# Rotary embedding, 1 core: all loads and stores on SyncE's one queue, in a written-out order

## The chip, the cores and the metric

The kernel runs on 1 core of one Trainium2 chip. The metric is the device time of an execution in microseconds (us). The program uses five engines: TensorE (PE), VectorE (DVE), ScalarE (ACT), GpSimd (POOL) and SyncE (SP). Transfers between HBM and SBUF are run by the core's 16 DMA engines; SP and ACT each issue theirs on a queue of their own (q1 is SP's in the profile, q10 is ACT's).

## The reference

```python
# x [8, 2048, 8, 64], cos and sin [2048, 32], all float32
def reference(x, cos, sin):
    x1 = x[..., : x.shape[-1] // 2]
    x2 = x[..., x.shape[-1] // 2 :]
    cos = cos[None, :, None, :]
    sin = sin[None, :, None, :]
    out1 = x1 * cos - x2 * sin
    out2 = x1 * sin + x2 * cos
    return np.concatenate([out1, out2], axis=-1)
```

x is 33.55 MB and so is the output; each table is 0.26 MB.

## The kernel before

The 2048 positions of a batch are laid over 128 partitions, 16 positions (`R`) to a partition, so that one batch is one tile `xt` of 128 x 8192 float32 (4 MB, `ROW` elements in a partition). `HD` is 512 elements (one position of all heads) and `UNIT` is 2048 (four positions). There are 8 batches and `NBUF` = 5 tiles: batches 0 to 4 are loaded ahead, and the load of batch 5 has to wait until the store of batch 0 has left its tile, that of 6 for the store of 1, that of 7 for the store of 2. Results are written back into the tile they came from, and stored from there. In the following, x5 stands for the load of batch 5 and s5 for its store.

`load` (L64) issues the loads on SP's queue: batch 0 in pieces of 1, 1 and 2 MB with the cos table behind the first of them (L69), every other batch in one transfer of 4 MB (L67). The sin table is loaded on ACT's queue (L76). `store` (L72) issues stores on ACT's queue (L74), those of the last batch on SP's. A queue's instructions are issued in the order of the program; where a transfer waits for a semaphore, all that its engine has behind it waits too. The names `keep(...)` put an instruction at its place in that order.

`rotate` (L102) works on one piece of a batch, mostly a `UNIT` (128 x 2048), and has three kinds. Kind A: GpSimd multiplies with sin and with minus sin (L122, two instructions of 128 x 1024), VectorE multiplies with cos (L129) and adds (L136). Kind B (first piece of batches 2, 4 and 5): the same products, the sum is made by TensorE with an identity matrix into PSUM (L143, L144) and copied back by ACT (L145). Kind C (first piece of batches 1 and 3): VectorE makes both products (L129, L148), TensorE the sums (L160, L161), ACT the copies (L165). The cos table is first copied to PSUM by VectorE (L93), sin to its negative and to PSUM by ACT (L90, L91).

The loop at L184 takes the batches in turn. `pieces` (L170) gives the pieces of a batch, `shares` (L177) how its store is cut: batch 0 into 512, 3584 and 4096 elements of a partition, the last batch into 4096, 2048 and 2048, the others whole. After batch b the load of batch b + 5 is issued:

```python
        if b + NBUF <= last:
            load(b + NBUF)
```

Of the kernel before, what the change touches and what calls it, by code (L numbers as in the profile page):

```python
# [10 lines left out]
def kernel(  # L11
# [7 lines left out]
    nc = tc.nc  # L19
    keep = tc.keep_in_program_order  # L20
# [6 lines left out]
    HD = H * D  # L27
    R = S // P
    ROW = R * HD
    UNIT = 4 * HD  # L30
    NBUF = 5
    C = 512
    last = B - 1

    xv = x.rearrange("b (q r) h d -> b q (r h d)", q=P)
    ov = out.rearrange("b (q r) h d -> b q (r h d)", q=P)
    cos_src = cos.rearrange("(q r) d -> q r d", q=P)
    sin_src = sin.rearrange("(q r) d -> q r d", q=P)
# [10 lines left out]
    sin_sb = const_pool.tile([P, R, Dh], f32, tag="sb")  # L49
# [6 lines left out]
    xts = {}  # L56

    def spans(sizes):
        lo = 0
        for n in sizes:  # L60
            yield lo, n
            lo += n

    def load(b):  # L64
        xt = xpool.tile([P, ROW], f32, tag="xt", name=f"xt{b}")
        for lo, n in spans([UNIT, UNIT, 2 * UNIT] if b == 0 else [ROW]):
            keep(nc.sync.dma_start(out=xt[:, lo : lo + n], in_=xv[b, :, lo : lo + n]))  # L67
            if b == 0 and lo == 0:
                keep(nc.sync.dma_start(out=cos_sb, in_=cos_src))  # L69
        xts[b] = xt  # L70

    def store(b, lo, n):  # L72
        queue = nc.sync if b == last else nc.scalar
        keep(queue.dma_start(out=ov[b, :, lo : lo + n], in_=xts[b][:, lo : lo + n]))  # L74

    keep(nc.scalar.dma_start(out=sin_sb, in_=sin_src))  # L76
    for b in range(NBUF):
        load(b)

# [2 lines left out]
        out=eye,  # L82
        in_=eye,
# [86 lines left out]
    def pieces(b):  # L170
        if b == 0:
            return [2 * HD, 2 * HD, UNIT, UNIT, UNIT]
        if b == last:
            return [UNIT, UNIT, UNIT, 2 * HD, 2 * HD]
        return [UNIT] * 4

    def shares(b):  # L177
        if b == 0:
            return [HD, 7 * HD, 2 * UNIT]
        if b == last:  # L180
            return [2 * UNIT, UNIT, UNIT]
        return [ROW]

    for b in range(B):  # L184
        done = 0
        outs = list(spans(shares(b)))
        for lo, n in spans(pieces(b)):
            rotate(b, lo, n)
            done = lo + n
            while outs and sum(outs[0]) <= done:  # L190
                store(b, *outs.pop(0))
        if b + NBUF <= last:
            load(b + NBUF)


# [28 lines left out]
```

## Time and profile before

| what | value |
|---|---|
| time, median of 3 runs | 163.59 us (163.51 to 164.44) |
| profiled execution: span from the first to the last instruction | 161.6 us (2.0 us below the median of the runs; no other time is listed for it) |
| busy: VectorE, GpSimd | 140.1 us (87%), 138.9 us (86%) |
| busy: TensorE, ScalarE | 47.1 us (29%), 12.8 us (8%) |
| moved by DMA | 67.65 MB, mean 419 GB/s over the span |
| time of the packets on 16 engines: SP's queue, ACT's queue | 55.3% of the span (38.01 MB), 42.9% (29.62 MB) |
| a load of 4 MB, issue to landing (median of 7) | 40.3 us |
| a store of 4 MB on ACT's queue, issue to landing (median of 6) | 28.3 us |

Busy shares are shares of the span. The time from issue to landing of a transfer holds the time it stands behind others in its queue and shares the engines with the other queue; it is not the time that its bytes need. The span is compared with spans, and the time with times.

### The profile page before, as it was taken

The page shows a single profiled execution, that of the slowest core. Times are in us where ns is not written, and L with a number is a line of the kernel's source. Part 1 is how long each engine was busy: PE and PEld are TensorE (multiplying, and loading weights), DVE is VectorE, ACT ScalarE, POOL GpSimd, SP SyncE. Part 2 cuts the span into 40 slices and gives each one's busy share as a digit, 9 for nine tenths or more (in the row PEclk, how much of TensorE's full clock was granted, in tenths as well). Part 3 has the DMA queues.
Part 4 walks back from the last instruction along what each step waited for, and adds up shares of the span by engine and source line. Part 5 has one row for each costly group of instructions (what it writes and reads, how often), then busy time and mean ns, then how long its engine had stood idle before and what let it go on. Part 6 is the DMA issues. An engine that isn't in the chain of part 4 may idle for free.

```text
span 161.6 us, 460 instructions
## 1 busy us (share of the span) xinstructions
PE 47.1 (29%) x80; PEld 17.8 (11%) x80; DVE 140.1 (87%) x66; ACT 12.8 (8%) x14; POOL 138.9 (86%) x70
## 2 busy tenths in 40 slices
PE   0000000597209750977039813972000000000000
PEld 0000000143004210322023302330000000000000
DVE  0297999999999999999999999699969999899920
ACT  3300000002200220022000120022000000000000
POOL 1399999999999999976999989997899979999500
PEclk9999999999965997599858995699555555555555
DMA  5999999999999999999999999999999999999995
GB/s 157 419 462 413 424 469 403 394 457 457 410 402 450 442 470 389 454 454 389 470 438 389 471 432 389 462 446 398 446 448 406 430 462 406 430 462 397 414 408 225
DMA packets 3458, 67.65 MB, mean 419 GB/s; under 512 B 384, under 2 KB 384, under 8 KB 768
## 3 DMA queue, kind: packets, MB, share of 16 engines
q1 hardware_dynamic: 2016, 38.01, 55.3%
q10 hardware_dynamic: 1440, 29.62, 42.9%
q14 instruction: 2, 0.02, 0.0%
HBM read 34.08 MB, written 33.55 MB: 419 GB/s over the span
## 4 chain that ended last, share of the span: by engine, by line
DVE 53%; DMA 29%; POOL 9%; issue 5%; DVEq 0%; SPq 0%; POOLq 0%
DVE t L129 28%; DMA xt<-in_x_dram 25%; DVE xt L136 22%; POOL t L122 9%; DMA sin_sb<-in_sin_dram 4%; DVE t L148 3%; DVEq L136 0%; SPq L67 0%; POOLq L122 0%
## 5 line engine op out<-in xcount | busy, mean ns | idle before, releaser
L122 POOL TENSOR_TENSOR t<-xt,sin_sb 128x1024 f32<-128x1024 f32 (+1 forms) x32 | 70.5, 2202 | 12.1 <-DMA xt<-in_x_dram 6.7
L129 DVE TENSOR_TENSOR t<-xt,cos_ps 128x2048 f32<-128x2048 f32 (+1 forms) x34 | 73.4, 2166 | 0.8
L122 POOL TENSOR_TENSOR t<-xt,nsin 128x1024 f32<-128x1024 f32 (+1 forms) x32 | 70.5, 2202 | 0.0
L136 DVE TENSOR_TENSOR xt<-t,t 128x2048 f32<-128x2048 f32 (+1 forms) x29 | 62.2, 2144 | 6.7 <-POOL t L122 4.1
L143 PE MATMUL o<-t,eye 128*128 128x512 f32 x24 | 15.9, 749 | 24.4 <-DVE t L129 21.0
L160 PE MATMUL o<-t,eye 128*128 128x512 f32 x16 | 11.2, 789 | 38.3 <-DVE t L129 36.1
L144 PE MATMUL o<-t,eye 128*128 128x512 f32 x24 | 14.7, 698 | 0.0
L145 ACT COPY xt<-o 128x1024 f32<-128x1024 f32 x6 | 6.1, 1012 | 45.7 <-PE o L144 45.7
L143 PEld LDWEIGHTS o<-t,eye 128*128 128x128 f32 x24 | 5.3, 247 | 33.6 <-issue 27.7
L160 PEld LDWEIGHTS o<-t,eye 128*128 128x128 f32 x16 | 3.7, 256 | 43.8 <-POOL t L122 30.2
L165 ACT COPY xt<-o 128x1024 f32<-128x1024 f32 x4 | 4.0, 1012 | 47.3 <-PE o L161 47.3
L93 DVE COPY cos_ps<-cos_sb 128x512 f32<-128x512 f32 x1 | 0.7, 694 | 7.0 <-DMA cos_sb<-in_cos_dram 7.0
L144 PEld LDWEIGHTS o<-t,eye 128*128 128x128 f32 x24 | 5.4, 227 | 7.4 <-issue 7.4
L161 PE MATMUL o<-t,neye 128*128 128x512 f32 x8 | 6.2, 863 | 0.2 <-DVE t L148 0.2
L148 DVE TENSOR_TENSOR t<-xt,sin_ps 128x2048 f32<-128x2048 f32 x2 | 4.6, 2280 | 0.0
L161 PE MATMUL o<-t,eye 128*128 128x512 f32 x8 | 4.1, 592 | 0.0
L161 PEld LDWEIGHTS o<-t,neye 128*128 128x128 f32 x8 | 1.8, 260 | 4.7 <-issue 3.0
L161 PEld LDWEIGHTS o<-t,eye 128*128 128x128 f32 x8 | 1.5, 190 | 1.9 <-issue 1.9
L90 ACT ACT_TABLE_LOAD x1 | 1.3, 1283 | 1.2 <-PEq L208 1.2
L90 ACT ACTIVATE nsin<-sin_sb 128x512 f32<-128x512 f32 x1 | 0.6, 630 | 4.1 <-DMA sin_sb<-in_sin_dram 4.1
L91 ACT COPY sin_ps<-sin_sb 128x512 f32<-128x512 f32 x1 | 0.6, 579 | 0.0
L80 POOL MEMSET eye<- 128x128 f32 x1 | 0.2, 205 | 0.3 <-POOLq L208 0.3
(6 smaller groups left out, 1.0 us busy)
## 6 DMA issues: line engine op xcount, KB each, us to landing
xt<-in_x_dram SPq DMA_DIRECT2D x7, 4096.0 KB, 40.3
out_dram<-xt ACTq DMA_DIRECT2D x6, 4096.0 KB, 28.3
xt<-in_x_dram SPq DMA_DIRECT2D x2, 1024.0 KB, 6.7
xt<-in_x_dram SPq DMA_DIRECT2D x1, 2048.0 KB, 12.4
out_dram<-xt ACTq DMA_DIRECT2D x1, 2048.0 KB, 25.9
out_dram<-xt SPq DMA_DIRECT2D x1, 2048.0 KB, 11.1
out_dram<-xt SPq DMA_DIRECT2D x2, 1024.0 KB, 7.5
out_dram<-xt ACTq DMA_DIRECT2D x1, 1792.0 KB, 20.8
```

Of the source, the lines that this page charges most:

```text
L90: keep(nc.scalar.mul(nsin, sin_sb, -1.0))
L93: keep(nc.vector.tensor_copy(cos_ps, cos_sb))
L122: nc.gpsimd.tensor_mul(out=t2u[:, :, u, :].rearrange("p (r h) d -> p r h d", h=H), in0=xu[:, :, 1 - u, :].rearrange("p (r h) d -> p r h d" ...
L129: nc.vector.tensor_mul(out=t1.rearrange("p (r k d) -> p r k d", r=nr, d=Dh), in0=xk, in1=rep(cos_ps[:, r0 : r0 + nr, :], 2 * H),)
L136: keep(nc.vector.tensor_add(out=xt, in0=t1, in1=t2))
L143: nc.tensor.matmul(oc, eye, t1[:, cs], start=True, stop=False)
L144: nc.tensor.matmul(oc, eye, t2[:, cs], start=False, stop=True)
L145: keep(nc.scalar.copy(xt[:, 2 * j * C : 2 * (j + 1) * C], o))
L148: nc.vector.tensor_mul(out=t2.rearrange("p (r k d) -> p r k d", r=nr, d=Dh), in0=xk, in1=rep(sin_ps[:, r0 : r0 + nr, :], 2 * H),)
L160: nc.tensor.matmul(oc, eye, t1u[:, gs, u, :], start=True, stop=False)
L161: nc.tensor.matmul(oc, eye if u else neye, t2u[:, gs, 1 - u, :], start=False, stop=True)
L165: nc.scalar.copy(xu[:, :, u, :], o.rearrange("p (g d) -> p g d", d=Dh))
```

## The change

The sin table is loaded on SP's queue, between the first piece of x and the cos table. All stores go to SP's queue. Batch 0 is stored by one transfer of 4 MB instead of three. The loads of batches 5, 6 and 7 are issued one batch later in the loop: after batch b (from 1 on) comes the load of batch b + 4, so that on SP's queue s1 stands ahead of x5, s2 ahead of x6 and s3 ahead of x7. The order of the other engines' arithmetic stays; ACT has no transfers left. Lines after L75 move up by one.

```diff
         for lo, n in spans([UNIT, UNIT, 2 * UNIT] if b == 0 else [ROW]):
             keep(nc.sync.dma_start(out=xt[:, lo : lo + n], in_=xv[b, :, lo : lo + n]))
             if b == 0 and lo == 0:
+                keep(nc.sync.dma_start(out=sin_sb, in_=sin_src))
                 keep(nc.sync.dma_start(out=cos_sb, in_=cos_src))
         xts[b] = xt
 
     def store(b, lo, n):
-        queue = nc.sync if b == last else nc.scalar
-        keep(queue.dma_start(out=ov[b, :, lo : lo + n], in_=xts[b][:, lo : lo + n]))
-
-    keep(nc.scalar.dma_start(out=sin_sb, in_=sin_src))
+        keep(nc.sync.dma_start(out=ov[b, :, lo : lo + n], in_=xts[b][:, lo : lo + n]))
+
     for b in range(NBUF):
         load(b)
...
     def shares(b):
         if b == 0:
-            return [HD, 7 * HD, 2 * UNIT]
+            return [ROW]
         if b == last:
             return [2 * UNIT, UNIT, UNIT]
         return [ROW]
...
             while outs and sum(outs[0]) <= done:
                 store(b, *outs.pop(0))
-        if b + NBUF <= last:
-            load(b + NBUF)
+        if b >= 1 and b + NBUF - 1 <= last:
+            load(b + NBUF - 1)
```

## The prediction, made before the changed kernel ran

> **What bounds the kernel now.** I read the DMA rows of the page first, because the kernel does little arithmetic per byte, and then asked the waits what each load and store stood behind.
>
> ```profile
> span 161.6 us, 460 instructions
> DMA  5999999999999999999999999999999999999995
> q1 hardware_dynamic: 2016, 38.01, 55.3%
> q10 hardware_dynamic: 1440, 29.62, 42.9%
> HBM read 34.08 MB, written 33.55 MB: 419 GB/s over the span
> ```
>
> The DMA row is at 9 in every slice but the two at the ends, and the two queues (q1 is SP's, q10 ACT's) fill 55.3 + 42.9 = 98.2% of the sixteen engines. Nothing is waiting for VectorE; the DMA engines have work from about 2 us to about 160.5 us. The chain of waits names VectorE for 53% of the span, and it misleads here: it follows back from the last instruction through one batch at a time and does not see that the store it ends with stood in a backlog. Next I asked for stages of different kinds (length, then the engines' busy times, clock, DMA share, GB/s):
>
> ```profile
> 6.00:24.00 18.00, 0.00 (x0) 0.00 (x0) 15.62 (x10) 1.35 (x3) 17.39 (x10) 1.00 1.03 435
> 54.00:130.00 76.00, 31.79 (x57) 12.12 (x56) 71.76 (x32) 8.10 (x8) 70.81 (x32) 0.76 1.01 434
> 134.00:146.00 12.00, 0.00 (x0) 0.00 (x0) 11.22 (x6) 0.00 (x0) 12.00 (x6) 0.50 0.99 426
> ```
>
> The first stage is nearly all loads, the second half loads and half stores, the third stores alone. The rate does not depend on the mix. (A view of 12 us counts a packet whole where it starts; sixteen packets of 32 KB are 0.52 MB, or 44 GB/s of such a view, so 426 is not a lower rate.) The packet records say it more sharply: a packet of 32 KB takes 1.213 us at the median in all three stages and on both queues, which is 16 x 32,768 B / 1.213 us = 432 GB/s. That is the ceiling that either kernel works against. The waits of SP's queue show the price of the two-queue order:
>
> ```profile
> SPq L67 <- DMA out_dram<-xt: 57.9, 3, 28.8
> SPq L74 <- DMA xt<-in_x_dram: 40.0, 1, 40.0
> SPq L67 <- DVE xt L136: 18.8, 1, 18.8
> ```
>
> Three loads stood for 57.9 us behind the stores that free their tile. It cost nothing, since the other queue kept the engines busy meanwhile, as the DMA row shows. The last load landed at 132.95 us, and the compute engines felt it little:
>
> ```profile
> POOL t L122 <- DMA xt<-in_x_dram: 6.7, 6, 2.3
> DVE xt L136 <- POOL t L122: 4.1, 4, 1.4
> ```
>
> **The sum of before.** From the packet records: the first packet starts at 1.86 us; all packets at their usual length take 157.04 us on sixteen engines; 1.40 us is packets that ran longer than usual (0.85 in the first 6 us, 0.23 at 22 to 26 us); the last packet ends at 160.51 us, so 0.2 is uneven ends. Landing and closing take 1.1 us. Together 1.86 + 157.04 + 1.40 + 0.2 + 1.1 = 161.6, the span. The median of the runs shown is 163.59, that is 2.0 above the span of the profiled execution, and I carry these 2.0 over.
>
> **The change, part by part.**
>
> *Bytes and packets.* No transfer is dropped; 24 DMAs become 22. Batch 0's store loses its pieces of 256 KB (128 packets of 0.084 us), 1792 KB (128 of 0.535) and 2 MB (128 of 0.611): 128 x 1.230 / 16 = 9.84 us. One store of 4 MB takes 128 x 1.213 / 16 = 9.70. Gain 0.14 us. The 0.23 us of long load packets at 22 to 26 us lie where the 256 KB store ends and the next begins; bounds 0 to 0.23, I take 0.2, since nothing else changes there.
>
> *Start.* The sin table moves from ACT's queue to SP's, behind the first piece of x. SP issues x, sin, cos, x in steps of about 0.45 us, so the fourth leaves at about 2.1 instead of 1.63 us; the first piece holds the engines until 1.86 + 0.85 + 2.47 = 5.2 us, so no gap: 0. Sin lands between 6.2 (x's end, 0.67 of its own, 0.35 to land) and 7.0 (with cos, as late as now), against 6.54. At worst GpSimd starts 0.5 us later; that is paid from compute slack below: 0. ACT loses ten issues of 0.34 us and is busy 8%: 0.
>
> *Order on one queue.* SP now issues x0 to x4, s0, s1, x5, s2, x6, s3, x7, s4, s5, s6 and three pieces of s7. A whole batch takes 9.70 us. Running it in order from 1.86 us with 0.85 of slow start: x4 ends at 52.7, s0 62.4, s1 72.1, x5 81.8, s2 91.5, x6 101.2, s3 110.9, x7 120.6, s4 130.3, s5 140.0, s6 149.7, s7 154.6, 157.1, 159.6. Each of these is now held against what it needs.
>
> - Loads that wait for a store. x5 needs s0 landed (62.4 + 0.35 = 62.8; the first piece of x landed 0.34 us after its last packet). Behind it on SP are s2 and all that follows; ahead of it s1, which holds the engines till 72.1. SP therefore issues x5 9.3 us before the engines run dry. From issue to first packet the trace shows 1.13 us on idle engines (0.73 to 1.86) and 3.55 us on busy ones (the store issued at 144.77, first packet 148.32). Both fit into 9.3: 0. x6 is covered by x5 and s2, x7 by x6 and s3. Uncovered, each would cost 0.35 + 1.13 = 1.48 us.
> - Stores that wait for compute. s0 to s5 were issued before at 27.9 (its last piece), 46.4, 62.6, 81.1, 97.3 and 114.7 us, all over 15 us ahead of their turn here. s6 was issued at 134.9; with 3.55 it is ready at 138.5 against 140.0. The pieces of s7 went at 144.8, 149.5 and 154.7, ready at 148.3, 153.1 and 158.2 against 149.7, 154.6 and 157.1: even with the compute of before only the last is late, by 1.1 us.
> - Compute. x5, x6 and x7 now land at about 82, 102 and 121 us; before, at 93.5, 113.6 and 133.0. GpSimd wants them near 92, 111 and 129. So the waits of VectorE for GpSimd after 100 us (1.22, 1.44 and 0.57 in the timeline) go, and the last piece is ready near 151.4 instead of 154.7. What is late next: nothing, the DMA queue is the limit. Gain on the end: 0.
>
> *Boundaries on one ring.* The trace shows load after load on one queue, and store after store, without a gap. It shows no load directly behind a store on a queue, nor the reverse; the new order has seven such boundaries. Bounds: 0 each, by load after load, to 1.48 each, if the engines drained as at an uncovered wait, 10.4 in all. I take 0, since mixed packets of two queues run at the same 1.213 us and load-to-load is the nearest row.
>
> The Trainium skill gives in "DMA: Bandwidth & Descriptors" ("Anatomy of one DMA") a fixed cost of about 2.0 us for a DMA, most of it the receipt of the last write, heaviest in HBM; that is stated for GpSimd's path. It speaks against a load that waits for a store: three uncovered waits would be 3 x 2.0 = 6.0 us by it. The trace has the last store landing some 0.3 us after its last packet, so the row is lower, and no run here yet shows an uncovered wait.
>
> Sum: -0.14 - 0.2 = -0.34 us; 161.6 - 0.3 = 161.3 for the span, 163.59 - 0.34 = 163.2 us for the time.
>
> **Rivals.** A difference of about 1% (1.6 us) is what a measurement of this kernel can tell from no change.
>
> - *Forecast: the DMA engines stay full, no change (0.78).* 163.2, from 162.4 to 164.3: up to 0.8 us of the 1.4 us of long packets goes besides, or the last store is late by its 1.1.
> - *Boundaries drain (slower, 0.12).* Seven changes of direction on one ring, at up to 1.48 us; at half price 163.2 + 5.2 = 168.4. It decides over 1% from (1.6 + 0.34) / 7 = 0.28 us each. For it: no row of before excludes it. Against it: the constant packet time.
> - *The cover fails (slower, 0.05).* x5, x6, x7 leave only after the engines ran dry: 3 x 1.48 = 4.4, 167.6 us. It needs s1 issued after 62.8 us; it was issued at 46.4, so 16 us of margin speak against it.
> - *Faster by over 1% (0.05).* If all 1.40 us of long packets and the 0.14 go: 163.59 - 1.54 = 162.05, just inside 1%. More needs packets under 1.213 us, and none of this size shows that.
> - That the scheduler undoes the order: the built program has SP's transfers in the order listed, and its waits are those counted above, so this has no chance of its own.
>
> **How the numbers follow.** The likeliest case gives 163.2. The range reaches down to 162.2, near the floor of 162.05, and up by a quarter of the boundary bound (2.6) to 165.8, leaving out the dearer boundaries, the failed cover and little else. Faster 0.05, same 0.78, slower 0.17.
>
> **What would show it.** In the profile after: one hardware queue with all 67.6 MB and near 98%; the DMA row at 9 in the same 38 slices; SP waiting for store landings two or three times with no dip in GB/s; VectorE's waits for GpSimd below 2 us; the last load landing near 121 us. A digit under 9 inside, every 20 us from 52 us on, means boundaries drain; GpSimd waiting long for x5 to x7 means the cover failed; packets below 1.2 us would prove the ceiling wrong.

## The result, and the profile after

The changed kernel takes 164.99 us (median of 15 runs, 163.75 to 165.61) against 163.72 us for the kernel before (15 runs beside it). The ratio is 1.0066, with a 95% interval of 1.0043 to 1.009: about 1.1 us slower. That is within the 1% the forecast called no change, but the interval excludes 1, and the forecast had the sign the other way (163.2 us, -0.34). The profiled execution took 164.72 us, with a span of 162.9 us against 161.6. The loss is not the same in every execution: five of the fifteen took 163.75 to 164.11 us.

These are the page's lines after; the second is the mean busy share of the DMA engines in 40 slices (tenths), the third the GB/s they moved in them:

```profile
span 162.9 us, 453 instructions
DMA  5999899899998999999999999999999999999993
GB/s 193 414 451 487 386 475 426 386 491 410 394 507 257 467 434 402 475 410 418 475 394 443 451 396 467 418 412 475 394 402 475 410 418 475 394 459 402 420 410 135
q1 hardware_dynamic: 3168, 67.63, 97.5%
HBM read 34.08 MB, written 33.55 MB: 415 GB/s over the span
```

All bytes go through q1 now and the engines are 97.5% busy, where two queues made 98.2%. The slices jump by some 40 GB/s anyway, since packets of 32 KB are counted whole where they start. One slice stands out: 257 GB/s at 49 to 53 us, where x4 ends and s0 begins. There is no such slice at the later changes of direction. The waits of SP's queue and of the compute engines:

```profile
SPq L74 <- DVE xt L135: 94.1, 9, 18.6
SPq L67 <- DMA out_dram<-xt: 38.4, 3, 17.5
```

```profile
POOL t L121 <- DVE xt L135: 2.6, 2, 2.2
DVE xt L135 <- POOL t L121: 0.9, 2, 0.7
```

SP waits for compute and for three stores, as planned, and no compute engine waits for a load of x any more: GpSimd's 6.7 us behind loads are gone, VectorE's waits for GpSimd fell from 4.1 to 0.9 us. The compute side improved as forecast and it is worth nothing. The end is where the time went (stage, its length, busy times of PE, PEld, DVE, ACT and POOL, granted clock, DMA share, GB/s), the kernel before first:

```profile
159.00:160.00 1.00, 0.00 (x0) 0.00 (x0) 0.00 (x0) 0.00 (x0) 0.00 (x0) 0.50 0.63 262
160.00:161.00 1.00, 0.00 (x0) 0.00 (x0) 0.00 (x0) 0.00 (x0) 0.00 (x0) 0.50 0.02 8
```

and the changed kernel:

```profile
159.00:160.00 1.00, 0.00 (x0) 0.00 (x0) 0.00 (x0) 0.00 (x0) 0.00 (x0) 0.50 0.87 369
160.00:161.00 1.00, 0.00 (x0) 0.00 (x0) 0.00 (x0) 0.00 (x0) 0.00 (x0) 0.50 0.20 82
161.00:162.00 1.00, 0.00 (x0) 0.00 (x0) 0.00 (x0) 0.00 (x0) 0.00 (x0) 0.50 0.04 16
```

In the last microseconds a share of 0.20 is about three of sixteen engines. The landing marks of the last store (one from each engine) have their median at 160.43 us against 160.18 in the kernel before, and the last of them at 161.94 against 160.75: most engines are done almost as early as before, a few are more than 1 us late, and the store has landed when the slowest is done.

The packet records give the same account that the prediction used. "Usual" is all data packets at their usual length over sixteen engines (the 4-byte packets that mark a landing, 0.2 to 0.4 us in all, are left out and so end up in "uneven"), "long" what packets took beyond that, both averaged over the engines; "uneven" is how far the last packet ends behind that sum. The remainder to the span, 1.2 to 1.3 us, is landing and closing.

| kernel | first packet | usual | long | uneven | last packet ends | span | ratio to before (95%) |
|---|---|---|---|---|---|---|---|
| before | 1.74 | 157.00 | 1.40 | 0.25 | 160.39 | 161.6 | |
| changed | 1.75 | 156.86 | 1.77 | 1.24 | 161.61 | 162.9 | 1.0066 (1.0043 to 1.009) |
| changed, second profile | 1.74 | 156.86 | 1.80 | 1.15 | 161.54 | 162.8 | 1.0079 (1.0058 to 1.01) |

Of the 1.3 us between the spans, +1.0 is unevenness, +0.4 long packets, -0.14 the fewer small packets, and the rest closing. The 0.4 is itself a difference: the first store behind x4 has 1.03 us of long packets at 48 to 54 us (0.23 at the first store before), while the first 6 us have 0.42 instead of 0.85.

### The profile page after: what moved, and what is told of

Same layout as the page of the kernel before. It is cut to its first block, busy times and chain, and to the rows that moved or that the text cites. A ratio compares the mean times of both kernels' runs of the same rounds, so it can differ in the third digit from the quotient of the medians.

```text
span 162.9 us, 453 instructions
## 1 busy us (share of the span) xinstructions
PE 47.0 (29%) x80; PEld 17.8 (11%) x80; DVE 140.1 (86%) x66; ACT 12.8 (8%) x14; POOL 138.8 (85%) x70
## 3 DMA queue, kind: packets, MB, share of 16 engines
q1 hardware_dynamic: 3168, 67.63, 97.5%
## 4 chain that ended last, share of the span: by engine, by line
DVE 72%; POOL 11%; issue 6%; DMA 3%; DVEq 0%; SPq 0%; POOLq 0%
DVE t L128 38%; DVE xt L135 31%; POOL t L121 11%; DMA sin_sb<-in_sin_dram 3%; DVE t L147 3%; DVEq L135 0%; SPq L67 0%; POOLq L121 0%
```

## The experiments

Four theories stood at the start. "Boundary": a store directly behind loads on one ring (what one queue has lined up on an engine) stalls engines, some more than others. "First write": the first large store of the program holds every engine up, and the old small pieces hid that. "Uneven engines on one ring": engines that fall behind are what counts, whatever holds them up. "Chance": the uneven end is an accident of one profile. Later "runs" (or "mixing") came up: what hurts is a long run of loads followed by stores, and loads and stores taken in turn don't stall.

**One edit at a time, two queues kept.** The kernel before with batch 0 stored by one transfer:

```diff
         if b == 0:
-            return [HD, 7 * HD, 2 * UNIT]
+            return [ROW]
```

> The kernel before with one edit: batch 0 is stored by one 4 MB transfer on ACT's queue (two queues, sin on ACT). Theory 'first write' (the first large store of the program holds every DMA engine up by about 0.9 us wherever it stands): long packets of about 0.9 us on sixteen engines where s0 starts (28 us), time +0.5 to +0.9 us over before. Theory 'boundary' (the stall belongs to a store directly behind a run of loads on the same ring): no such place, time within 0.3 us of before.

Measured: 1.0018 (1.0003 to 1.0033). Long packets of 0.71 us on average per engine do appear at 27 to 32 us, where s0 starts, yet uneven is 0.27 and the span 161.6. The first write does stall the engines, and that hardly moves the time. The kernel before with only the sin table moved to SP's queue:

```diff
-    keep(nc.scalar.dma_start(out=sin_sb, in_=sin_src))
...
             if b == 0 and lo == 0:
+                keep(nc.sync.dma_start(out=sin_sb, in_=sin_src))
                 keep(nc.sync.dma_start(out=cos_sb, in_=cos_src))
```

> The kernel before with one edit: the sin table on SP's queue behind the first piece of x, as in the changed kernel. Two queues and the three pieces of batch 0's store stay. If the parts add up (single store of batch 0 alone 1.0018, with sin moved as well 1.0005), moving sin is worth about -0.2 us: ratio 0.997 to 1.000, and this version would be the quickest of all. If the single store's loss was chance, ratio 1.000 to 1.002.

Measured: 1.0008 (0.9995 to 1.0022). No gain; the hope that the parts add up to a quicker version failed. Its profile has 0.71 us of long packets around the start of s0, though s0 goes in the three old pieces there. So the 0.23 us in the one profile of before was probably a low sample, and not the merit of the pieces.

**The one queue undone.** The changed kernel with the stores of batches 0 to 6 on ACT's queue:

```diff
     def store(b, lo, n):
-        keep(nc.sync.dma_start(out=ov[b, :, lo : lo + n], in_=xts[b][:, lo : lo + n]))
+        queue = nc.sync if b == last else nc.scalar
+        keep(queue.dma_start(out=ov[b, :, lo : lo + n], in_=xts[b][:, lo : lo + n]))
```

> The changed kernel with the stores of batches 0 to 6 on ACT's queue: order, sin and the single store of batch 0 as changed, only the one queue is undone. Theory 'boundary' and theory 'uneven engines on one ring': the loss goes, time within 0.3 us of before (ratio 0.998 to 1.002). Theory 'first write': s0 still stalls at 28 us, ratio about 1.004.

Measured: 1.0005 (0.9994 to 1.0016), uneven 0.52. This interval and that of the changed kernel don't overlap; the single edit is the queue of seven stores (and with it the order in which loads and stores reach the engines). Putting them on SP's one queue costs the 0.6%, about 1.0 us; the single store and the sin table together cost 0.3 us at most, by this interval. Its profile still has the first store's stall (0.94 us at 27 to 32, the slice of 275):

```profile
GB/s 182 413 449 485 413 405 485 275 477 429 388 485 421 396 494 405 396 494 405 405 494 396 421 471 396 461 445 388 469 431 405 461 429 405 469 429 392 429 409 202
```

```profile
159.00:160.00 1.00, 0.00 (x0) 0.00 (x0) 0.00 (x0) 0.00 (x0) 0.00 (x0) 0.50 0.76 320
160.00:161.00 1.00, 0.00 (x0) 0.00 (x0) 0.00 (x0) 0.00 (x0) 0.00 (x0) 0.50 0.06 25
```

The engines finish together here: 0.06 in the microsecond where the changed kernel shows 0.20.

**Is it the first write?** The changed kernel with 256 KB of batch 0 stored early on ACT's queue, and, in the next, with the old three pieces on SP's one queue:

```diff
+        queue = nc.scalar if b == 0 and lo == 0 else nc.sync
+        keep(queue.dma_start(out=ov[b, :, lo : lo + n], in_=xts[b][:, lo : lo + n]))
...
         if b == 0:
-            return [ROW]
+            return [HD, 15 * HD]        # in the next: [HD, 7 * HD, 2 * UNIT], all on nc.sync
```

> The changed kernel, but the first 256 KB of batch 0's output are stored early (10 us) on ACT's queue, beside the loads; the rest of batch 0 (3840 KB) follows on SP's queue as one transfer. Theory 'first write': the first write is paid under the loads and the dip at 49 to 53 us goes, time 0.7 to 1.0 us below the changed kernel (about 164.0). Theory 'boundary': the dip stays at 49 to 53 us, time as the changed kernel, 164.5 to 165.2.

> The changed kernel with batch 0's store in its three old pieces (256 KB, 1792 KB, 2 MB), all on SP's one queue behind x4. Theory 'boundary' and theory 'first write' both keep the stall at 49 to 53 us, ratio to before 1.004 to 1.009. If the size of the first store's packets makes it (2 KB here against 32 KB), the dip goes and the ratio falls to 1.001.

Measured: 1.007 (1.0049 to 1.0091) and 1.0071 (1.0052 to 1.009). A small early store does not take the stall away (0.90 us still at 48 to 54), nor do small pieces at its head (0.69), and the time stays. Both profiles have further long packets at the ends of x5, x6 and x7, where a store stands next, but in different forms. With the early store, 0.21, 0.12 and 0.35 us on average per engine, spread over many packets, with 2.19 long and 0.44 uneven in all; with the pieces, 0.04, 0.15 and 0.08 us, fewer packets, of up to 0.66, with 1.69 long and 1.74 uneven. Then batch 0's store alone was taken back to ACT's queue, in its old pieces:

```diff
+        queue = nc.scalar if b == 0 else nc.sync
+        keep(queue.dma_start(out=ov[b, :, lo : lo + n], in_=xts[b][:, lo : lo + n]))
...
-            return [ROW]
+            return [HD, 7 * HD, 2 * UNIT]
```

> The changed kernel with batch 0's store alone taken back to ACT's queue in its three old pieces; all else on SP's queue, where s1 then is the first store behind x4. If the stall at 49 to 53 us belongs to the first store of the program, it shrinks to the 0.3 us of before and the ratio falls to 1.001 to 1.004. If it belongs to the first store behind loads on that ring, it moves to s1 (52 to 55 us) and the ratio stays at 1.005 to 1.009.

Measured: 1.0102 (1.0074 to 1.013). Half of this expectation came true: the stall moved with s0 to 21 to 27 us (0.51 us of long packets), and s1, now the first store behind x4 on SP's ring, has none at 49 to 53. So the stall belongs to the program's first large store, wherever that stands. But the time did not fall, it rose: uneven 2.13, the most of all versions whose transfers keep 128 partitions. With the two-queue runs above, which have the stall at 1.0005 and 1.0018, this says that the first store's stall is not the loss. Why this mixture ends most unevenly stays open.

**Is it chance?** The changed kernel again:

> The changed kernel itself, for a second profile and for its time beside the other runs of this call. Both theories: ratio 1.004 to 1.009. Theory 'boundary' (a store directly behind a load on the one ring stalls engines, some more than others): again about 1 us of long packets at 48 to 54 us, shorter ones near 82, 101 and 121 us, and the DMA engines done at different times, 1 to 2 us apart, at the end. Theory 'chance': the uneven end of the first profile does not come back.

Measured: 1.0079 (1.0058 to 1.01), uneven 1.15 against 1.24. "Chance" falls.

```profile
160.00:161.00 1.00, 0.00 (x0) 0.00 (x0) 0.00 (x0) 0.00 (x0) 0.00 (x0) 0.50 0.22 90
161.00:162.00 1.00, 0.00 (x0) 0.00 (x0) 0.00 (x0) 0.00 (x0) 0.00 (x0) 0.50 0.02 8
```

Both profiles also say when the engines part. Every transfer leaves sixteen landing marks, one from each engine; the slowest engine lands this far behind the median (us):

| transfer | s1 | x5 | s2 | x6 | s3 | x7 | s4 | last piece of s7 |
|---|---|---|---|---|---|---|---|---|
| changed | 0.20 | 0.63 | 0.38 | 0.78 | 0.66 | 1.54 | 1.52 | 1.52 |
| second profile | 0.21 | 0.40 | 0.19 | 0.98 | 0.64 | 1.40 | 1.38 | 1.38 |

Read along the stores, the lag rises twice, by s3 and by s4, and from s4 on it stays within 0.02 us to the end, so it looks as if each engine has its fixed share of every transfer and nothing takes a late engine's work off it. What shows at x5 is mostly gone by s2. In the kernel before, the last piece of s7 is 0.58 behind.

The rise by s3 has a source that is not the change of direction: an instruction fetch of 8 KB on q14 at 94 us, while x6 is under way. The records do not name the engine, but on an engine a packet begins within 5 ns of the end of the one before it, so that an engine can be followed by its times. The engine that serves this fetch loses 0.31 us to it and 0.53 to a long packet right behind. It does so with two queues as well: 0.31 + 0.54 in the kernel before, and 0.31 + 0.35 with seven stores on ACT's queue, where that engine has no long packet afterwards.

The rise by s4 comes only with the one queue. Where x7 ends, between 119 and 123 us of the changed kernel, two packets run 0.55 and 0.70 us long and eight others lose 0.04 to 0.19; the one of 0.55 is on the engine that served the fetch at 94 us. In the second profile that same engine has packets 0.35 us long at the end of x6 and 0.54 at the end of x7, and it is the one that is done last. So this engine's delay is 0.84 us of fetch, which both kernels have, and 0.89 us of long packets at the ends of two loads, which the one queue adds. That being late already is what makes an engine's last load packets long would fit these two profiles, but no run here takes the fetch away.

**How many places, or how long the runs?** First two of the four places taken away, by the order s0, s1, s2, x5, x6, x7, s3:

```diff
-        if b >= 1 and b + NBUF - 1 <= last:
-            load(b + NBUF - 1)
+        if b == 2:
+            for nb in (5, 6, 7):
+                load(nb)
```

> The changed kernel with the order x0 to x4, s0, s1, s2, x5, x6, x7, s3 and so on: 2 places where a store follows a load instead of 4. Theory 'boundary' with a like cost each: ratio 1.003 to 1.005, no long packets near 82 and 101 us. Theory 'mixing': longer runs, ratio 1.008 or more.

Measured: 1.0053 (1.004 to 1.0066), long 1.57, uneven 0.78; the first store apart, the only long packets near a change of direction are 0.06 us on average at 110 to 112 (up to 0.39 in one packet), where x7 ends and s3 begins. This is just above what "boundary" expected (1.003 to 1.005) and well under the 1.008 of "mixing", although the runs of one direction are longer here. But its interval overlaps both of the changed kernel's, so that two places fewer cost less is likely (164.18 against 164.60 us beside it) and not shown. Then the opposite, thirteen places instead of four (the whole loads and stores of these batches go, and the loop over batches has, after the pieces):

```diff
+        if b in (2, 3, 4):
+            nb = b + 3
+            xts[nb] = xpool.tile([P, ROW], f32, tag="xt", name=f"xt{nb}")
+            for lo, n in spans([UNIT] * 4):
+                keep(nc.sync.dma_start(out=xts[nb][:, lo : lo + n], in_=xv[nb, :, lo : lo + n]))
+                store(b, lo, n)
```

> The changed kernel with x5 and s2, x6 and s3, x7 and s4 cut in quarters of 1 MB and taken in turn on the one queue: 13 places where a store follows a load instead of 4, same bytes. Theory 'boundary': each adds 0.1 to 0.3 us on some engines, ratio 1.010 to 1.020. Theory 'mixing' (the loss comes from long runs of one direction, and the two-queue kernel is quick because it mixes): the loss shrinks, ratio 1.002 to 1.005.

Measured: 1.0102 (1.0089 to 1.0115), just where "boundary" began, but the profile says why, and it is not that: packets of 8 KB raise the usual time from 156.86 to 157.97, 1.1 us, which is 0.7% by itself. Long packets are down to 1.37, uneven to 0.16, the lowest of all; beyond the first store hardly a packet is long at the other twelve places. A control with the same quarters, all four of a load ahead of all four of a store, follows:

```diff
             for lo, n in spans([UNIT] * 4):
                 keep(nc.sync.dma_start(out=xts[nb][:, lo : lo + n], in_=xv[nb, :, lo : lo + n]))
-                store(b, lo, n)
+            for lo, n in spans([UNIT] * 4):
+                store(b, lo, n)
```

> Control of the interleaved quarters: x5, x6, x7, s2, s3, s4 are cut into the same column quarters of 1 MB (8 KB packets, 1.1 us more packet time), but all four of a load go before all four of a store, as in the changed kernel; 4 places where a store follows a load. Theory 'runs' (a store behind a long run of loads stalls engines; taken in turn it doesn't): packet cost and stalls add up, ratio 1.012 to 1.016, uneven end 1 to 2 us. Theory 'packet size' (8 KB packets never stall): as the interleaved quarters, 1.010, uneven end below 1 us.

Measured: 1.0141 (1.0126 to 1.0156), long 1.69, uneven 0.48. Same bytes, same packets, same queue; runs cost 0.4% more than turns, and the intervals don't overlap. The uneven end stayed under the 1 us that "runs" had named, so part of the expectation missed, but long and uneven together are 2.17 against 1.53. That is as much as the ratios differ by (0.64 us), partly by luck: 0.19 of it lies in the first 6 us and at the first store, where the two kernels are alike, and each profile is of the shortest of four executions. The difference is shown by the times; what in the profile makes it up is not settled.

The last microseconds of the interleaved quarters and of the control (DMA share and GB/s at the right):

```profile
160.00:161.00 1.00, 0.00 (x0) 0.00 (x0) 0.00 (x0) 0.00 (x0) 0.00 (x0) 0.50 0.45 188
161.00:162.00 1.00, 0.00 (x0) 0.00 (x0) 0.00 (x0) 0.00 (x0) 0.00 (x0) 0.50 0.00 0
```

```profile
160.00:161.00 1.00, 0.00 (x0) 0.00 (x0) 0.00 (x0) 0.00 (x0) 0.00 (x0) 0.50 0.72 303
161.00:162.00 1.00, 0.00 (x0) 0.00 (x0) 0.00 (x0) 0.00 (x0) 0.00 (x0) 0.50 0.06 25
```

In the first the engines stop together, in the second a few go on.

**Turns without small packets.** To keep 32 KB packets, the transfers were cut by partitions instead of columns, quarters of 32 and halves of 64:

```diff
+            for p in range(0, P, 32):       # 64 in the second
+                rs = slice(p, p + 32)
+                keep(nc.sync.dma_start(out=xts[nb][rs, :], in_=xv[nb, rs, :]))
+                keep(nc.sync.dma_start(out=ov[b, rs, :], in_=xts[b][rs, :]))
```

> The changed kernel with x5 and s2, x6 and s3, x7 and s4 cut into quarters by partitions (32 partitions, packets stay 32 KB) and taken in turn on the one queue. Theory 'runs': no stalls and no packet cost, ratio 1.000 to 1.003, uneven end below 1 us. Theory 'packet size': stalls as in the changed kernel or more of them, ratio 1.006 to 1.012. If 32 partitions alone can't feed 16 engines, packets get longer than 1.213 us and the ratio goes over 1.02.

> As the quarters by partitions, with halves of 64 partitions (2 MB): 7 places where a store follows a load. Theory 'runs': between the quarters and whole batches, ratio 1.001 to 1.005. Theory 'boundary' with a like cost for each place: more than the changed kernel, ratio 1.009 to 1.013.

Measured: 1.1652 (1.1603 to 1.17) and 1.1883 (1.1841 to 1.1925). The last condition of the first expectation came true, and neither run tells anything of the theories, since transfers of fewer partitions are slow in themselves. The halves' profile has the same queue at full rate with 128 partitions and at two thirds of it with 64:

```profile
20.00:50.00 30.00, 11.70 (x18) 4.42 (x19) 29.38 (x14) 2.02 (x2) 30.00 (x15) 0.92 1.00 431
75.00:150.00 75.00, 19.43 (x34) 7.16 (x32) 55.66 (x25) 5.06 (x5) 51.45 (x23) 0.66 1.00 283
```

The engines are busy all the while (share 1.00), but the packets of 32 KB take 1.21 to 2.59 us there (median 1.46) instead of 1.213.

No version was quicker than the kernel before.

**What the runs show and what stays open.** Shown: the loss comes with loads and stores on one queue, and not with the first store, the sin table or compute; with the same packets on one queue, whole loads followed by whole stores cost 0.4% more than turns of 1 MB. Seen in the profiles of the changed kernel: packets run long at the ends of loads with a store behind them, and single engines fall 1.4 to 1.5 us behind; on the one that could be followed to the end, 0.84 us of the delay is an instruction fetch that both kernels have and 0.89 us are such packets. In the run with a small early store the same places cost about as much with less unevenness, so the uneven end is one form of the loss and not the only one. Open: what in an engine makes the last packets of a load run long when a store stands next in its ring, and whether two rings would stall too if they held the same unmixed runs, which was not tried.

## Why the prediction was right or wrong

- *The bound* was right: the DMA engines set the time. "Usual" fell from 157.00 to 156.86, the 0.14 us worked out. (The prediction's 157.04 held two small instruction fetches, and its zero for the packet records was 0.12 us off: the first packet starts at 1.74, not 1.86. Neither moves the sum.)
- *Loads that wait for a store, counted 0*: right. Three waits of 38.4 us in all, and no slice of low GB/s at 63, 73 or 93 us. x5, x6 and x7 landed at 83.4, 103.0 and 123.1 against 82, 102 and 121.
- *Compute, gain 0*: right. The last store was issued at 151.7 us (forecast 151.4), and it stood in a backlog.
- *Start, 0*: right. First packet at 1.75 us, and GpSimd's wait for sin is 4.9 us instead of 5.3.
- *The 0.2 us of long packets at 22 to 26 that was to go*: wrong in sign. They were put down to the 256 KB store. Every profile has such a stall where its first large store begins, 0.2 us in that of before and 0.5 to 1.0 in all others (1.03 in the changed kernel); one profile was taken for the rule. All long packets together went from 1.40 to 1.77, up 0.37 instead of down 0.2.
- *Boundaries on one ring, taken as 0*: this is the step that failed, and with it the next. The bounds 0 to 1.48 us each were right to be kept, but the value was chosen by load after load, and by a mean packet time of mixed queues, which has no such boundary in it. The rival "boundaries drain" named the place and missed the form: it is not a pause of all engines at seven places. All engines lose time at the first store, which they do with two queues too (0.7 to 0.9 us in three of those profiles, without the loss). At the three later places where a store follows a load some packets run long, 0.01 to 0.20 us a place on average over the engines in the two profiles, but up to 0.70 us on a single engine; and hardly any lie where a load follows a store. Moving seven stores off the one queue brought the ratio back to 1.0005.
- *Uneven ends, carried over at 0.2*: this is the term that was mis-sized. The sum averaged sixteen engines and took the spread of before as given. It went from 0.25 to 1.24, and that is 1.0 of the 1.3 us between the spans.
- Three of the signs named in advance came (one queue near 98%, SP's three waits for stores without a dip, VectorE's waits under 2 us). The last load landed 2 us later than the 121 named, and the DMA row has three slices at 8 inside instead of none. The sign for boundaries, a digit under 9 every 20 us, was too coarse. An engine that is 1 us late takes 0.06 us off a mean over sixteen, which no slice of 4 us shows.

The Trainium skill says in "DMA: Bandwidth & Descriptors" ("Issuing engines are not separate DMA queues") that issuing from several engines saves only the issue time, since all transfers run on the same sixteen engines. The rate agrees (1.213 us a packet on either). The time does not quite: seven stores moved to the other queue took the ratio from 1.0066 to 1.0005.

## What to carry to other kernels

When the DMA engines are the bound, as here, the mean busy share and the mean rate are not the whole sum: the last store lands when the slowest engine is done, so look at the last microseconds and at how far apart the engines finish. In this kernel a load queue and a store queue that both have work waiting ran 0.6% quicker than one in-order queue with whole loads and then whole stores. Breaking up the runs on the one queue helped only against the same small packets; the smaller packets (1.0102 in all) and the fewer partitions (1.1652 and 1.1883) cost more than it gave. Making compute earlier, or waits shorter, is worth nothing while a transfer's backlog covers them.

## What the hardware showed that was not expected

- Transfers of 64 of the 128 partitions ran at 283 GB/s against 431, with packets of up to 2.59 us, about twice 1.213. It looks as if two engines then at times share what each has to itself with 128; that is argued, not shown. The Trainium skill ("DMA: Bandwidth & Descriptors", "Rules for kernel authors") advises one transfer of 128 partitions over two of 64 because both run on the same engines; the runs agree with the advice and add that the rate falls as well.
- The first large store of a program made packets long by 0.2 to 1.0 us on average per engine, in every profile of these kernels, on either queue and with or without a small store ahead.
- Each of these profiles has two instruction fetches of 8 KB on q14 within the span, one at 94 to 97 us and one between 100 and 134 us. In the kernel before, the engine that serves the first is held for 0.31 us, and its next packet ran 0.54 us longer than usual. In the second profile of the changed kernel, where that engine is the last one done, this is 0.84 us of its delay.
